# Three rotary operations from VectorE to GpSimd in another form, and the last output bank summed as two halves

## Chip, cores and metric

One core of a Trainium2 chip runs the whole layer. The metric is the device time of one execution in microseconds (us). Five engines work side by side, each with its own queue, which it takes in order: TensorE (PE, its weight loads PEld), VectorE (DVE), ScalarE (ACT), GpSimd (POOL) and SyncE (SP), which issues most of the loads and stores. TensorE writes its results into PSUM, which is used here as eight banks of 128 x 512 floats.

## What is computed

One decoder layer on 256 tokens of width 1024. All of it is float32.

```python
xn = rms_norm(h, norm_mix_g)
proj = jnp.einsum('bsd,de->bse', xn, w_in)
qa, ka, va, c_q, c_kv, k_rope = jnp.split(proj, cuts, axis=-1)
...   # head group A: dilated window attention on rms-normed qa, ka; va
...   # head group B: queries and keys from the latents c_q, c_kv, plus the shared k_rope;
qb = jnp.concatenate([qb[..., :64], apply_rope(qb[..., 64:], positions)], axis=-1)
kb = jnp.concatenate([kb[..., :64], apply_rope(kb[..., 64:], positions)], axis=-1)
...
h = h + jnp.einsum('bse,ed->bsd', mixed, w_o)
hn = rms_norm(h, norm_ffn_g)
hid = jnp.square(jax.nn.relu(jnp.einsum('bsd,df->bsf', hn, w_ff1)))
h = h + jnp.einsum('bsf,fd->bsd', hid, w_ff2)
```

`apply_rope` needs the cosine and the sine of position times frequency, 256 x 16 angles each.

## The kernel before

The 256 tokens are two tiles of 128 rows (`NT = 2`, index t). Every product is made of three: activations and weights are split into a high part (`his`, `hi`) and a low remainder (`los`, `lo`), and high x high, low x high and high x low are summed in one PSUM bank. Weights come from HBM in chunks (tile `raw`, three buffers), are cut into pieces of up to 1024 columns, and each piece is split by a ScalarE cast (L254) and a VectorE subtraction (L255) into one of five `his` and one of five `los` buffers. A load waits until VectorE has subtracted the last piece of the chunk that held the buffer.

PSUM is shared out as three pools: `acc` (4 banks), `mm` (2) and `sc` (2). The projections sum in `acc` (some in `sc`), transposes go through `mm`, attention scores through `sc`.

TensorE's work up to the feed-forward part is kept in the order of a table written by hand, of which this is the stretch that matters:

```python
c1*5 A1 r0 c1*3 l*2 L0 l*3 x0 l*2 L1 l x1 g*2 y0 x2 g*2 y1 g L2 x3
```

`c1` is a step of the second half of the c_q projection, `l` a step of the c_kv projection, `g` of the va projection (each step six matmuls). `A1` (`stack_heads(1)`) transposes the normed keys of head group A through the two `mm` banks (L163), casts their high part (ACT, L517) and subtracts it for the low part (DVE, L518, four instructions; the first and the third read one bank, the second and the fourth the other). `L0` and `L1` transpose the c_q latent through the same two banks, and split it (ACT L286, DVE L287). `x0`, `x1` are score products with their softmax (DVE L546 and L552, ACT L549), `y0` transposes the first unit's probabilities, so it waits for L552.

`r0` is `rotary_tables`: it reduces the angles by multiples of two pi, folds them into the range where a polynomial holds, and evaluates it, nearly all on GpSimd, on tiles of 128 x 32 (`ang`, `arg`) and 128 x 64 (`sq`, `trig`). GpSimd is kept in program order. Three of the folds, an absolute value (L421), a minimum (L424) and a maximum (L426), stand on VectorE. GpSimd goes on from the tables to the norms of the latents and the rotation of the shared key (`kr`), and then to the factors `s_k`, whose input VectorE makes.

VectorE's and ScalarE's order is set by the framework's scheduler, from its own estimate of times; the kernel gives none. A VectorE instruction that waits for GpSimd holds up all that stands behind it in VectorE's queue.

The feed-forward part goes over 8 blocks of 512 hidden columns: `ff1(n)`, then `ff2(n-1)`, which adds to four banks `f_ps[t][b]` (two of `sc`, two of `mm`; t the rows, b the column half of the output). The last block, `ff2_last(7)`, finishes one bank after the other: twelve matmuls of 512 columns, then VectorE multiplies the bank by the norm's factor and adds the residual (L813), then SP stores it (L814). The last bank, t = b = 1, is added and stored in two halves of 256 columns, after all twelve matmuls.

Of the kernel before, what the change touches and what calls it, by code (L numbers as in the profile page):

```python
# [20 lines left out]
ALU = mybir.AluOpType  # L21
AX = mybir.AxisListType

P = 128
S = 256
NT = S // P
# [11 lines left out]
NFB = DFF // FB  # L38
# [139 lines left out]
def tile_layer(ctx, tc, x, xt, cols_in, rows_in, w_all, out):  # L178
    nc = tc.nc
    V, A, G, T = nc.vector, nc.scalar, InOrder(tc, nc.gpsimd), Products(tc)  # L180
# [14 lines left out]
    acc = ctx.enter_context(tc.tile_pool(name="acc", bufs=4, space=bass.MemoryType.PSUM))  # L195
# [3 lines left out]
    def bank(pool=mm):  # L199
        return pool.tile([P, 512], F32, name=pool.name)  # L200
# [4 lines left out]
    def tiny(n, name, bufs=1):  # L205
        return small.tile([P, n], F32, name=name, bufs=bufs)
# [8 lines left out]
    first = const.tile([P, NFRONT + S], F32, name="first")  # L215
# [4 lines left out]
    xs = [keep.tile([P, DM], F32, name=f"x{t}") for t in range(NT)]  # L220
# [26 lines left out]
    def split_next():  # L247
        i = queue["split"]
        c, r, a, n = PIECES[i]
        while queue["load"] <= c:  # L250
            list(load_next())
        raw = queue["raw"][c][:, r:r + a, :]
        hi, lo = (p.tile([P, PIECE], F32R, name=p.name)[:, :a * n].rearrange("p (a n) -> p a n", a=a) for p in (his, los))
        pinned(A.copy(out=hi, in_=raw))  # L254
        pinned(V.tensor_tensor(out=lo, in0=raw, in1=hi.bitcast(F32), op=ALU.subtract))  # L255
        queue["parts"][i] = hi, lo
        queue["split"] += 1

    def weights(name):

        i = queue["at"]
        assert CHUNKS[PIECES[i][0]][0] == name, (PIECES[i], name)
        if queue["split"] == i:
            split_next()
        queue["at"] += 1
        return queue["parts"].pop(i)
# [41 lines left out]
    def three(outs, act, w, k, j, first, last, cs=slice(None)):  # L308

        hi, lo = act[:2]  # L310
        whi, wlo = (z[:, j, cs] for z in w)
        for i, (a, z) in enumerate(((hi, whi), (lo, whi), (hi, wlo))):
            for t in range(NT):
                T.matmul(out=outs[t][:, :whi.shape[1]], lhsT=a[:, k, t * P:(t + 1) * P], rhs=z, start=first and i == 0, stop=last and i == 2)

    def project_steps(name, act, k0, n, done, pool=acc):


        ps = [bank(pool) for _ in range(NT)]
        j = 0  # L320
        while j < n:
            w = weights(name)
            for i in range(w[0].shape[1]):
                three(ps, act, w, k0 + j, i, j == 0, j == n - 1)
                j += 1
                if j == n:
                    done(ps)
                yield
# [62 lines left out]
    def rotary_tables():  # L391
        ang = [const.tile([P, NT, HR], F32, name=f"ang{i}") for i in range(4)]
        pos = const.tile([P, NT], F32, name="pos")
        V.tensor_copy(out=pos, in_=first[:, F_POS:F_POS + NT].bitcast(I32))
        a0, kh, kl, r = ang
        full = [P, NT, HR]
        inv = first[:, F_INV:F_INV + HR]
        G.tensor_tensor(out=a0, in0=pos.unsqueeze(2).broadcast_to(full), in1=inv.unsqueeze(1).broadcast_to(full), op=ALU.mult)

        def two_step(out, in0, scalar, in1, op0, op1):  # L400
            tmp = tiny(NT * ROPE, "rot2", bufs=2)[:, :math.prod(in0.shape[1:])]
            tmp = tmp.rearrange("p (t f) -> p t f", t=NT) if len(in0.shape) == 3 else tmp
            G.tensor_scalar(out=tmp, in0=in0, scalar1=scalar, scalar2=None, op0=op0)
            G.tensor_tensor(out=out, in0=tmp, in1=in1, op=op1)

        def turns(out, in_, period):
            G.tensor_scalar(out=out, in0=in_, scalar1=1.0 / period, scalar2=MAGIC, op0=ALU.mult, op1=ALU.add)
            G.tensor_scalar(out=out, in0=out, scalar1=MAGIC, scalar2=None, op0=ALU.subtract)

        def less(out, in_, k, part):  # L410
            two_step(out=out, in0=k, scalar=-part, in1=in_, op0=ALU.mult, op1=ALU.add)

        turns(kh, a0, 2 * math.pi * 4096)
        for part in TWO_PI_HI[:3]:
            less(a0, a0, kh, part)
        less(r, a0, kh, TWO_PI_HI[3])
        turns(kl, r, 2 * math.pi)
        for k, part in ((kl, TWO_PI[0]), (kh, TWO_PI_HI[3]), (kl, TWO_PI[1]), (kh, TWO_PI_HI[4]), (kl, TWO_PI[2]), (kh, TWO_PI_HI[5])):
            less(a0, a0, k, part)
        arg = const.tile([P, NT, 2, HR], F32, name="arg")  # L420
        V.scalar_tensor_tensor(out=r, in0=a0, scalar=-1.0, in1=a0, op0=ALU.mult, op1=ALU.max)  # L421
        G.tensor_scalar(out=arg[:, :, 0, :], in0=r, scalar1=-1.0, scalar2=math.pi / 2, op0=ALU.mult, op1=ALU.add)
        G.tensor_scalar(out=r, in0=a0, scalar1=-1.0, scalar2=math.pi, op0=ALU.mult, op1=ALU.add)
        V.tensor_tensor(out=a0, in0=a0, in1=r, op=ALU.min)  # L424
        G.tensor_scalar(out=r, in0=a0, scalar1=-1.0, scalar2=-math.pi, op0=ALU.mult, op1=ALU.add)
        V.tensor_tensor(out=arg[:, :, 1, :], in0=a0, in1=r, op=ALU.max)  # L426
        af = arg.rearrange("p t c f -> p (t c f)")
        sq = const.tile([P, NT * ROPE], F32, name="sq")
        trig = const.tile([P, NT, 2, HR], F32, name="trig")
        tf = trig.rearrange("p t c f -> p (t c f)")  # L430
        G.tensor_tensor(out=sq, in0=af, in1=af, op=ALU.mult)
        G.tensor_scalar(out=tf, in0=sq, scalar1=SIN[6], scalar2=None, op0=ALU.mult)
        for c in SIN[5:0:-1]:
            two_step(out=tf, in0=tf, scalar=c, in1=sq, op0=ALU.add, op1=ALU.mult)
        two_step(out=tf, in0=tf, scalar=1.0, in1=af, op0=ALU.add, op1=ALU.mult)
        for i in range(2):
            tab_c = const.tile([P, NT, ROPE], F32, name=f"tabc{i}")
            tab_s = const.tile([P, NT, ROPE], F32, name=f"tabs{i}")
            g1, g2 = (cols[:, C_ROPE + i * ROPE + z * HR:C_ROPE + i * ROPE + (z + 1) * HR].unsqueeze(1).broadcast_to(full) for z in range(2))
            cos, sin = trig[:, :, 0, :], trig[:, :, 1, :]  # L440
            G.tensor_tensor(out=tab_c[:, :, 0:HR], in0=cos, in1=g1, op=ALU.mult)
            G.tensor_tensor(out=tab_c[:, :, HR:], in0=cos, in1=g2, op=ALU.mult)
            two_step(out=tab_s[:, :, 0:HR], in0=sin, scalar=-1.0, in1=g2, op0=ALU.mult, op1=ALU.mult)
            G.tensor_tensor(out=tab_s[:, :, HR:], in0=sin, in1=g1, op=ALU.mult)
            tabs.append((tab_c, tab_s))
# [273 lines left out]
    for b in range(2):  # L719
# [3 lines left out]
    single = {  # L723
        "A": stack_heads,
        "r": lambda i: rotary_tables(),
        "b": lambda i: spread_bias(),
        "x": begin_a,
# [23 lines left out]
    f_ps, hid = [], {}  # L751
# [40 lines left out]
    def ff2(n):  # L792
        if n == 0:
            f_ps.extend([bank(pool) for _ in range(2)] for pool in (sc, mm))
        for kk in range(4):
            w = weights("ff2")
            for b in range(2):
                three([f_ps[t][b] for t in range(NT)], hid[n], w, kk, 0, n + kk == 0, False, slice(b * 512, (b + 1) * 512))

    def ff2_last(n):  # L800

        ws = [weights("ff2") for _ in range(4)]
        hi, lo = hid[n]
        for b in range(2):
            for t in range(NT):
                ts, cs = slice(t * P, (t + 1) * P), slice(b * 512, (b + 1) * 512)
                for kk, (whi, wlo) in enumerate(ws):
                    for i, (a, w) in enumerate(((hi, whi), (hi, wlo), (lo, whi))):
                        T.matmul(out=f_ps[t][b], lhsT=a[:, kk, ts], rhs=w[:, 0, cs], start=False, stop=kk == 3 and i == 2)
                cut = 256 if b == t == 1 else 512  # L810
                for c0 in range(0, 512, cut):
                    o = xs[t][:, b * 512 + c0:b * 512 + c0 + cut]
                    V.scalar_tensor_tensor(out=o, in0=f_ps[t][b][:, c0:c0 + cut], scalar=r2[:, t:t + 1], in1=o, op0=ALU.mult, op1=ALU.add)  # L813
                    nc.sync.dma_start(out=out[ts, b * 512 + c0:b * 512 + c0 + cut], in_=o)  # L814

    ssh = tiny(NT, "ssh")
    for n in range(NFB):
        ff1(n)
        if n == 1:
# [4 lines left out]
            r2 = tiny(NT, "r2")  # L824
            rsqrt(r2, ssh, NT)
            G.tensor_tensor(out=r2, in0=r2, in1=r2, op=ALU.mult)
        if n:
            ff2(n - 1)
    ff2_last(NFB - 1)


# [44 lines left out]
```

## Time and profile before

| | |
|---|---|
| time, median of 3 runs (lowest to highest) | 320.17 us (319.86 to 320.26) |
| the profiled execution, and its span in the trace | 320.45 us, 318.6 us |
| TensorE busy | 311.2 us (98%) |
| VectorE busy | 215.7 us (68%) |
| ScalarE busy | 177.9 us (56%) |
| GpSimd busy | 57.8 us (18%) |
| mean DMA rate over the span | 179 GB/s |
| mean granted TensorE clock | 0.994 of full speed |

The span runs from the first to the last instruction in the trace; the execution's time has 1.85 us around it. "Busy" of TensorE includes ends that are modelled, since matmuls overlap: two matmuls of 512 columns start 0.23 us apart and each is drawn 0.39 us long. The granted clock is the share of 2.4 GHz that TensorE was given; 0.50 is its lower level, 1.2 GHz.

### The profile page before, as it was taken

The page shows a single profiled execution, that of the slowest core. Times are in us where ns is not written, and L with a number is a line of the kernel's source. Part 1 is how long each engine was busy: PE and PEld are TensorE (multiplying, and loading weights), DVE is VectorE, ACT ScalarE, POOL GpSimd, SP SyncE. Part 2 cuts the span into 40 slices and gives each one's busy share as a digit, 9 for nine tenths or more (in the row PEclk, how much of TensorE's full clock was granted, in tenths as well). Part 3 has the DMA queues.
Part 4 walks back from the last instruction along what each step waited for, and adds up shares of the span by engine and source line. Part 5 has one row for each costly group of instructions (what it writes and reads, how often), then busy time and mean ns, then how long its engine had stood idle before and what let it go on. Part 6 is the DMA issues. An engine that isn't in the chain of part 4 may idle for free.

```text
span 318.6 us, 4545 instructions
## 1 busy us (share of the span) xinstructions
PE 311.2 (98%) x1646; PEld 266.8 (84%) x1646; DVE 215.7 (68%) x387; ACT 177.9 (56%) x317; POOL 57.8 (18%) x118
## 2 busy tenths in 40 slices
PE   8999997999999999999999999999999999999995
PEld 7887997888988887888888888888888888888883
DVE  3859949987797995637995574774754845846722
ACT  4876657858786774419574454443643643545400
POOL 4045877770372200001000000000000000000000
PEclk9999997999999999999999999999999999999999
DMA  7996992434462561305568565646556465553002
GB/s 225 398 385 192 320 291 77 148 86 145 164 220 67 192 205 66 134 0 189 209 242 286 151 219 174 237 146 217 180 151 244 145 233 168 185 195 132 0 35 99
DMA packets 12326, 56.95 MB, mean 179 GB/s; under 512 B 1384, under 2 KB 3440, under 8 KB 7696
## 3 DMA queue, kind: packets, MB, share of 16 engines
q1 hardware_dynamic: 10560, 54.94, 50.6%
q10 hardware_dynamic: 1744, 1.73, 1.8%
q8 instruction: 13, 0.21, 0.3%
q14 instruction: 9, 0.07, 0.1%
HBM read 55.07 MB, written 1.06 MB: 176 GB/s over the span
## 4 chain that ended last, share of the span: by engine, by line
PE 83%; DVE 5%; POOL 5%; ACT 3%; issue 2%; DVEq 0%; ACTq 0%
PE acc L160 45%; PE sc L160 19%; PE mm L160 15%; PE mm L163 4%; DVE los L255 2%; POOL s_a L174 2%; POOL ang L174 2%; ACT his L254 2%; POOL rot L174 1%; ACT sqs L376 1%; DVE big L518 1%; DVE s_a L472 0%; DVE two L287 0%; DVE half L785 0%; ACT two L286 0%
## 5 line engine op out<-in xcount | busy, mean ns | idle before, releaser
L255 DVE TENSOR_TENSOR los<-raw,his 128x1024 fp32r<-128x1024 f32 (+3 forms) x106 | 121.1, 1150 | 64.5 <-ACT his L254 64.4
L254 ACT CAST his<-raw 128x1024 fp32r<-128x1024 f32 (+3 forms) x106 | 104.2, 991 | 86.7 <-PE acc L160 46.1
L160 PE MATMUL acc<-his,two 128*128 128x512 f32 (+2 forms) x288 | 74.4, 381 | 0.0
L160 PE MATMUL acc<-two,his 128*128 128x512 f32 x240 | 63.1, 393 | 0.2 <-DVE half L785 0.2
L160 PEld LDWEIGHTS acc<-his,two 128*128 128x128 f32 x288 | 52.0, 195 | 6.7 <-issue 0.8
L160 PE MATMUL mm<-his,big 128*128 128x512 f32 x128 | 49.1, 390 | 0.0
L160 PE MATMUL sc<-his,big 128*128 128x512 f32 x128 | 49.0, 389 | 0.0
L160 PEld LDWEIGHTS acc<-two,his 128*128 128x128 f32 x240 | 42.6, 188 | 7.6 <-DVE half L785 0.4
L160 PE MATMUL acc<-los,two 128*128 128x512 f32 (+2 forms) x144 | 41.4, 369 | 0.0
L160 PEld LDWEIGHTS acc<-two,los 128*128 128x128 f32 x240 | 34.5, 190 | 3.4
L160 PE MATMUL acc<-two,los 128*128 128x256 f32 x240 | 35.8, 282 | 0.0
L160 PEld LDWEIGHTS acc<-los,two 128*128 128x128 f32 x144 | 27.0, 193 | 3.7
L160 PEld LDWEIGHTS mm<-his,big 128*128 128x128 f32 x128 | 24.0, 188 | 4.8
L160 PEld LDWEIGHTS sc<-his,big 128*128 128x128 f32 x128 | 24.1, 188 | 4.8
L160 PE MATMUL sc<-los,big 128*128 128x512 f32 x64 | 24.9, 389 | 0.0
L160 PE MATMUL mm<-los,big 128*128 128x512 f32 x64 | 24.9, 389 | 0.0
L549 ACT ACTIVATE half<-half,mx 128x128 f32<-128x128 f32 (+1 forms) x32 | 14.2, 449 | 2.3 <-DVE mx L546 2.3
L784 ACT COPY half<-acc 128x256 f32<-128x256 f32 x30 | 9.8, 374 | 7.8 <-PE acc L160 7.8
L160 PEld LDWEIGHTS mm<-los,big 128*128 128x128 f32 x64 | 12.0, 188 | 2.5
L160 PEld LDWEIGHTS sc<-los,big 128*128 128x128 f32 x64 | 12.0, 188 | 2.5
L788 ACT CAST big<-half 128x512 fp32r<-128x512 f32 x16 | 10.0, 625 | 4.1 <-DVE half L786 4.1
L785 DVE TENSOR_TENSOR half<-acc,half 128x256 f32<-128x256 f32 x30 | 11.4, 418 | 1.3 <-ACT half L784 1.3
(143 smaller groups left out, 317.2 us busy)
## 6 DMA issues: line engine op xcount, KB each, us to landing
raw<-in_weights_dram SPq DMA_DIRECT2D x36, 1024.0 KB, 4.8
raw<-in_weights_dram SPq DMA_DIRECT2D x13, 512.0 KB, 5.6
raw<-in_weights_dram SPq DMA_DIRECT2D x6, 768.0 KB, 4.5
raw<-in_weights_dram SPq DMA_DIRECT2D x2, 576.0 KB, 7.6
x<-in_x_dram SPq DMA_DIRECT2D x2, 512.0 KB, 8.7
big<-vec_d ACTq DMA_DIRECT2D x1, 1024.0 KB, 11.9
big<-in_xt_dram SPq DMA_DIRECT2D x3, 256.0 KB, 7.2
raw<-in_weights_dram SPq DMA_DIRECT2D x2, 384.0 KB, 3.0
```

The lines of the kernel that those rows point to most:

```text
L160: return self._issue(self.tc.nc.tensor.matmul(**kw))
L163: return self._issue(self.tc.nc.tensor.transpose(**kw))
L174: return lambda *a, **kw: self.tc.keep_in_program_order(op(*a, **kw))
L254: pinned(A.copy(out=hi, in_=raw))
L255: pinned(V.tensor_tensor(out=lo, in0=raw, in1=hi.bitcast(F32), op=ALU.subtract))
L376: return A.activation(out=junk[:, :src.shape[1]], in_=src, func=AF.Square, accum_out=dst)
L518: V.tensor_tensor(out=k_st[other, :, i, ts], in0=t3[rs], in1=k_st[rs, :, i, ts].bitcast(F32), op=ALU.subtract)
L549: A.activation(out=sb[:, i, :], in_=sb[:, i, :], func=AF.Exp, scale=-1.0, bias=mx[:, i:i + 1], accum_out=mx[:, 4 + i:5 + i])
L784: A.copy(out=zs, in_=ps[2 * b + i][:, S:])
L785: V.tensor_tensor(out=zs, in0=ps[2 * b + i][:, 0:S], in1=zs, op=ALU.add)
L788: A.copy(out=ht[:, sl, :], in_=s3)
```

## The change

The diff has two parts, and one line in a helper that lets a sum end for some rows alone.

In `rotary_tables` the three VectorE instructions go. The absolute value is made on GpSimd as 2 max(a, 0) - a (two instructions), the minimum of a and r as a - max(a - r, 0) (three), the maximum of a and r as a + max(r - a, 0) (three). So VectorE has three instructions less and GpSimd eight more, all of 128 x 32.

In the last block, the bank `f_ps[1][1]` is closed one block earlier (`last = (1,)` at n = 6): VectorE adds it to the residual at the start of `ff2_last`, and the last block's part of these outputs is summed afresh in two `acc` banks, 256 columns in each, one after the other. Each half is added and stored when its own twelve matmuls are done.

```diff
-                T.matmul(..., start=first and i == 0, stop=last and i == 2)
+                T.matmul(..., start=first and i == 0, stop=(t in last if isinstance(last, tuple) else last) and i == 2)
...
-        V.scalar_tensor_tensor(out=r, in0=a0, scalar=-1.0, in1=a0, op0=ALU.mult, op1=ALU.max)
+        G.tensor_scalar(out=kh, in0=a0, scalar1=0.0, scalar2=2.0, op0=ALU.max, op1=ALU.mult)
+        G.tensor_tensor(out=r, in0=kh, in1=a0, op=ALU.subtract)
         G.tensor_scalar(out=arg[:, :, 0, :], in0=r, scalar1=-1.0, scalar2=math.pi / 2, op0=ALU.mult, op1=ALU.add)
         G.tensor_scalar(out=r, in0=a0, scalar1=-1.0, scalar2=math.pi, op0=ALU.mult, op1=ALU.add)
-        V.tensor_tensor(out=a0, in0=a0, in1=r, op=ALU.min)
+        G.tensor_tensor(out=r, in0=a0, in1=r, op=ALU.subtract)
+        G.tensor_scalar(out=r, in0=r, scalar1=0.0, scalar2=None, op0=ALU.max)
+        G.tensor_tensor(out=a0, in0=a0, in1=r, op=ALU.subtract)
         G.tensor_scalar(out=r, in0=a0, scalar1=-1.0, scalar2=-math.pi, op0=ALU.mult, op1=ALU.add)
-        V.tensor_tensor(out=arg[:, :, 1, :], in0=a0, in1=r, op=ALU.max)
+        G.tensor_tensor(out=r, in0=r, in1=a0, op=ALU.subtract)
+        G.tensor_scalar(out=r, in0=r, scalar1=0.0, scalar2=None, op0=ALU.max)
+        G.tensor_tensor(out=arg[:, :, 1, :], in0=a0, in1=r, op=ALU.add)
...
-                three([f_ps[t][b] for t in range(NT)], hid[n], w, kk, 0, n + kk == 0, False, ...)
+                last = (1,) if b == 1 and n == NFB - 2 and kk == 3 else False
+                three([f_ps[t][b] for t in range(NT)], hid[n], w, kk, 0, n + kk == 0, last, ...)
...
+        add(f_ps[1][1], 1, 512, 512)
+        for t, c0, w in ((0, 0, 512), (1, 0, 512), (0, 512, 512), (1, 512, 256), (1, 768, 256)):
+            ts, cs = slice(t * P, (t + 1) * P), slice(c0, c0 + w)
+            ps = f_ps[t][c0 // 512] if w == 512 else bank(acc)[:, :w]
+            for kk, (whi, wlo) in enumerate(ws):
+                for i, (a, z) in enumerate(((hi, whi), (hi, wlo), (lo, whi))):
+                    T.matmul(out=ps, lhsT=a[:, kk, ts], rhs=z[:, 0, cs], start=w < 512 and kk == i == 0, stop=kk == 3 and i == 2)
+            nc.sync.dma_start(out=out[ts, cs], in_=add(ps, t, c0, w))
```

In the built programs the lines behind the new ones have moved by seven (L518 is L525, L598 is L605). VectorE's queue around the rotary operations, as a difference of the two programs (`big<-mm,big` are the four low parts of the keys, `los` the splits of c_kv weights):

```order
 L255 TENSOR_TENSOR los<-raw,his 128x576 x3
-L421 SCALAR_TENSOR_TENSOR ang_565<-ang_562 128x32
-L424 TENSOR_TENSOR ang_562<-ang_562,ang_565 128x32
-L518 TENSOR_TENSOR big<-mm,big 64x4x128
-L426 TENSOR_TENSOR arg<-ang_562,ang_565 128x2x16
-L518 TENSOR_TENSOR big<-mm,big 64x4x128
+L525 TENSOR_TENSOR big<-mm,big 64x4x128 x2
 L255 TENSOR_TENSOR los<-raw,his 128x576
-L518 TENSOR_TENSOR big<-mm,big 64x4x128 x2
-L598 COPY nats<-acc 128x384 x2
+L525 TENSOR_TENSOR big<-mm,big 64x4x128 x2
+L605 COPY nats<-acc 128x384 x2
```

Nothing between the third split and the four low parts of the keys is left on VectorE; the rest of this stretch keeps its order. GpSimd's queue at the same place:

```order
 L174 TENSOR_TENSOR ang_562<-rot_600,ang_562 128x32
+L174 TENSOR_SCALAR ang_563<-ang_562 128x32
+L174 TENSOR_TENSOR ang_565<-ang_563,ang_562 128x32
 L174 TENSOR_SCALAR arg<-ang_565 128x2x16
-L174 TENSOR_SCALAR ang_565<-ang_562 128x32 x2
+L174 TENSOR_SCALAR ang_565<-ang_562 128x32
+L174 TENSOR_TENSOR ang_565<-ang_562,ang_565 128x32
+L174 TENSOR_SCALAR ang_565<-ang_565 128x32
+L174 TENSOR_TENSOR ang_562<-ang_562,ang_565 128x32
+L174 TENSOR_SCALAR ang_565<-ang_562 128x32
```

Two of the five new instructions of this piece make the absolute value, three the minimum; three more follow for the maximum, and the polynomial (`sq`, `trig`) stands behind them as before. VectorE's last instructions, with the residual `x` of the rows t = 0 (x_112) and t = 1 (x_113):

```order
 L255 TENSOR_TENSOR los<-raw,his 128x1024 x2
-L813 SCALAR_TENSOR_TENSOR x_112<-sc,r_1882,x_112 128x512
-L813 SCALAR_TENSOR_TENSOR x_113<-mm,r_1882,x_113 128x512
-L813 SCALAR_TENSOR_TENSOR x_112<-sc,r_1882,x_112 128x512
-L813 SCALAR_TENSOR_TENSOR x_113<-mm,r_1882,x_113 128x256 x2
-L872 UNCONDITIONAL_BRANCH
+L813 SCALAR_TENSOR_TENSOR x_113<-mm,r_1887,x_113 128x512
+L813 SCALAR_TENSOR_TENSOR x_112<-sc,r_1887,x_112 128x512
+L813 SCALAR_TENSOR_TENSOR x_113<-mm,r_1887,x_113 128x512
+L813 SCALAR_TENSOR_TENSOR x_112<-sc,r_1887,x_112 128x512
+L813 SCALAR_TENSOR_TENSOR x_113<-acc,r_1887,x_113 128x256 x2
```

One addition of 512 columns is new, ahead of the others; the last two read two `acc` banks instead of one `mm` bank. On TensorE the last twelve matmuls of 512 columns become 24 of 256; all its work ahead of them stands in the same order in both programs.

## Rows read from the trace of the kernel before

**Rows 1.** Waits of TensorE from 64 to 315 us: total us, times, longest
```profile
PE mm L163 <- DVE half L552: 0.5, 1, 0.5
PE acc L160 <- DVE half L785: 0.2, 1, 0.2
```

**Rows 2.** TensorE in order of time, 51 to 64 us: start, us, instruction [idle before]
```profile
51.15 1.27 PE L163 MATMUL mm<-ident,nats 128*128 128x128 f32 x6 [1.78 <-DVE big L518]
...
55.94 1.00 PE L160 MATMUL sc<-big,two 128*128 128x128 f32 x8
...
57.63 0.69 PE L160 MATMUL acc<-his,two 128*128 128x288 f32 x4
...
58.42 0.82 PE L163 MATMUL mm<-ident,nats 128*128 128x128 f32 x6
59.00 0.78 PE L160 MATMUL acc<-his,two 128*128 128x288 f32 x4
...
63.80 0.82 PE L163 MATMUL mm<-ident,half 128*128 128x128 f32 x4 [0.53 <-DVE half L552]
```

**Rows 3.** VectorE in order of time, the same columns, 46 to 64 us
```profile
46.81 0.19 DVE L421 SCALAR_TENSOR_TENSOR ang<-ang 128x32 f32<-128x32 f32 x1 [2.92 <-POOL ang L174]
47.65 0.19 DVE L424 TENSOR_TENSOR ang<-ang,ang 128x32 f32<-128x32 f32 x1 [0.64 <-POOL ang L174]
47.87 0.69 DVE L518 TENSOR_TENSOR big<-mm,big 64x512 fp32r<-64x512 f32 x1
...
63.38 0.87 DVE L552 TENSOR_SCALAR half<-half,mx 128x128 f32<-128x128 f32 x4
```

**Rows 4.** ScalarE in order of time, the casts ahead of the first two L518
```profile
44.25 1.06 ACT L517 CAST big<-mm 64x512 fp32r<-64x512 f32 x2 [1.15 <-PE mm L163]
```

**Rows 5.** Stretches: length, busy us of PE PEld DVE ACT POOL, PEclk, DMA share, GB/s
```profile
47.87:63.38 15.51, 13.62 (x84) 12.39 (x82) 14.98 (x36) 12.19 (x32) 12.06 (x28) 0.89 0.35 115
...
52.10:55.00 2.90, 2.90 (x14) 2.90 (x13) 2.87 (x4) 2.67 (x7) 2.65 (x4) 0.50 0.28 113
...
64.00:65.00 1.00, 1.00 (x9) 0.88 (x9) 0.71 (x5) 1.00 (x5) 0.51 (x3) 1.00 0.85 78
```

**Rows 6.** GpSimd in order of time, 46 to 82 us
```profile
46.52 0.25 POOL L174 TENSOR_TENSOR ang<-rot,ang 128x32 f32<-128x32 f32 x1
...
48.86 0.29 POOL L174 TENSOR_TENSOR sq<-arg 128x64 f32<-128x64 f32 x1 [0.72 <-DVE arg L426]
...
52.74 1.42 POOL L174 TENSOR_SCALAR rot<-trig 128x64 f32<-128x64 f32 x1
...
58.15 0.47 POOL L174 TENSOR_TENSOR tabc<-trig,cols 128x32 f32<-128x32 f32 x2
...
71.35 0.37 POOL L174 TENSOR_SCALAR kr<-kr,by_kr 128x32 f32<-128x32 f32 x1
81.89 0.28 POOL L174 TENSOR_SCALAR s_k<-s_k,add_k 128x4 f32<-128x4 f32 x1 [10.17 <-DVE s_k L472]
```

**Rows 7.** VectorE's weight splits, two stretches: ns min/median/max, first and last start
```profile
L255 DVE TENSOR_TENSOR los<-raw,his x5: 1214/1226/1227, 52.7 to 62.2; 128x1024 fp32r<-128x1024 f32 x5
...
L255 DVE TENSOR_TENSOR los<-raw,his x54: 1214/1226/1227, 159.5 to 299.2; 128x1024 fp32r<-128x1024 f32 x54
```

**Rows 8.** TensorE and VectorE in order of time, feed-forward part and end
```profile
176.00 1.12 PE L160 MATMUL acc<-two,los 128*128 128x256 f32 x8
176.95 2.00 PE L160 MATMUL acc<-two,his 128*128 128x512 f32 x8
...
308.15 0.75 DVE L813 SCALAR_TENSOR_TENSOR x<-sc,r,x 128x512 f32<-128x512 f32 x1 [4.97 <-PE sc L160]
...
311.95 0.39 PE L160 MATMUL mm<-his,big 128*128 128x512 f32 x1
...
314.44 0.39 PE L160 MATMUL mm<-his,big 128*128 128x512 f32 x1
...
314.87 0.88 DVE L813 SCALAR_TENSOR_TENSOR x<-mm,r,x 128x256 f32<-128x256 f32 x2 [1.97 <-PE mm L160]
```

More of the change, by code (lines that the diff above doesn't have):

```diff
@@ L313, in three @@
             for t in range(NT):
-                T.matmul(out=outs[t][:, :whi.shape[1]], lhsT=a[:, k, t * P:(t + 1) * P], rhs=z, start=first and i == 0, stop=last and i == 2)
+                T.matmul(out=outs[t][:, :whi.shape[1]], lhsT=a[:, k, t * P:(t + 1) * P], rhs=z, start=first and i == 0, stop=(t in last if isinstance(last, tuple) else last) and i == 2)
     def project_steps(name, act, k0, n, done, pool=acc):
@@ L797, in ff2, with add @@
             for b in range(2):
-                three([f_ps[t][b] for t in range(NT)], hid[n], w, kk, 0, n + kk == 0, False, slice(b * 512, (b + 1) * 512))
+                last = (1,) if b == 1 and n == NFB - 2 and kk == 3 else False
+                three([f_ps[t][b] for t in range(NT)], hid[n], w, kk, 0, n + kk == 0, last, slice(b * 512, (b + 1) * 512))
     def ff2_last(n):
+        def add(ps, t, c0, w):
+            o = xs[t][:, c0:c0 + w]
+            V.scalar_tensor_tensor(out=o, in0=ps, scalar=r2[:, t:t + 1], in1=o, op0=ALU.mult, op1=ALU.add)
+            return o
         ws = [weights("ff2") for _ in range(4)]
         hi, lo = hid[n]
[L804 to L814, printed above, removed]
+        add(f_ps[1][1], 1, 512, 512)
[6 more added lines that the diff above has]
+            nc.sync.dma_start(out=out[ts, cs], in_=add(ps, t, c0, w))
     ssh = tiny(NT, "ssh")
```

## The prediction

> **What bounds the kernel now.** TensorE is busy for 98% of the span, so first I looked for where it is not: the list of its waits. From 64 us on there is next to nothing, 0.5 us for L552 and 0.2 us for L785 [rows 1], the first of which is the wait at 63.80 itself. So after 64 us the time is TensorE's own work in a fixed order, and whatever makes TensorE reach that point earlier makes the end earlier by as much, as long as the engines that feed it come earlier too. The other large wait lies before it: 1.78 us ahead of the transposes at 51.15, released by L518 [rows 2].
>
> Next I read VectorE's queue backwards from that L518. VectorE stands idle for 2.92 us, from 43.89 to 46.81, until GpSimd has an angle ready for L421, again for 0.64 us ahead of L424, and only then comes the first L518 at 47.87 [rows 3]. The low parts of the keys have nothing to do with the angles; they stand behind them in one queue. Their own inputs were there long before: ScalarE's first two casts took 44.25 to 45.31 [rows 4].
>
> Third, the granted clock. Behind that stall TensorE runs at 0.50, its lower level of 1.2 GHz, for 52.10 to 55.00 at least [rows 5]. From the start of the transposes at 51.15 to the start of the scores at 55.94 it needs 4.79 us [rows 2]; that is six transposes and three c_kv steps. At full clock six transposes take 0.58 (58.42 to 59.00) and a step 0.79 (57.63 to 58.42) [rows 2], together 0.58 + 3 x 0.79 = 2.95. So the low clock costs 1.84 us more, and stall and clock together 1.78 + 1.84 = 3.62 us.
>
> Fourth, what is late next. Between the first L518 at 47.87 and L552 at 63.38, VectorE is busy for 14.98 of 15.51 us [rows 3, 5]. So in this stretch VectorE, not TensorE, sets when the first probabilities are ready, and TensorE already waits 0.53 us for them at 63.80 [rows 2]. The gain is therefore the smaller of two: what TensorE saves before 63.80, and what VectorE saves before 63.38.
>
> **The rotary part, on VectorE.** Removed ahead of L552: idle 2.92 + 0.64 and three instructions, two of 0.19 by their rows and a third of the same shape and, by choice, the same length [rows 3], together 4.13 us. What comes back: VectorE is through at 43.89 and the first cast ends about half way through the pair, 44.25 + 0.53, call it 44.85 [rows 4], so it still idles some 0.97. That leaves 3.16. The second L518 then wants the second cast, done at 45.31; the first L518, 0.69 long [rows 3], covers that. Some of the 0.53 us that VectorE is idle between 47.87 and 63.38 [rows 5] may go as well, so VectorE saves 3.16 to 3.69; new short waits for ScalarE could take 0.3 off the lower end. I take 3.3, near the lower end, since the casts and the scores that feed VectorE here come from engines that are now no further ahead than before. L552 then starts at 63.38 - 3.3 = 60.1 and the transposes behind it at 63.80 - 3.3 = 60.5.
>
> On TensorE the stall goes entirely: the third and fourth L518, for which the two banks wait, come some 3 us earlier, the stall is 1.78. Without it I count on no drop of the clock there. TensorE would then reach the transposes of the probabilities 3.62 us earlier, 0.32 more than VectorE, and wait 0.53 + 0.32 = 0.85 us in place of 0.53. If VectorE were not the limit, TensorE could gain at most 3.62 + 0.53 = 4.15. So this part is worth 3.3 us, between 2.9 and 4.15.
>
> **The rotary part, on GpSimd.** Eight instructions of 128 x 32 more. One takes 0.25 us (46.52) where VectorE is idle, and the longest of this helper here 1.42 us (52.74) [rows 6]; I take 0.35 from start to start, nearer the first since they are of its shape. The three waits for VectorE go. Now the stretch from 46.77 to the polynomial at 48.86 takes 2.09; with eleven instructions it takes 11 x 0.35 = 3.85, so all behind it is 1.8 us later. What covers this: GpSimd finishes the shared key at 71.35 + 0.37 and is then idle for 10.17 us until VectorE delivers for `s_k` [rows 6]. VectorE will deliver 3.3 us earlier, so 6.9 us of cover are left, and 1.8 costs nothing. Without that cover each of these microseconds would be one of the end.
>
> VectorE now has work beside GpSimd where it was idle. Its weight splits take 1214 to 1227 ns in 52.7 to 62.2, where GpSimd is busy for most of the time, and the same 1214 to 1227 ns from 159.5 us on, where GpSimd has nothing to do [rows 5, 7]; so I charge VectorE nothing. The Trainium skill speaks against that ("SBUF — State Buffer", Who interferes with whom): of a VectorE instruction with two SBUF inputs and a GpSimd instruction that reads SBUF, the one that comes second is held until the first is done. In the trace the GpSimd half agrees (0.25 against 1.42 us), the VectorE half is not to be seen in these splits. By the rows the term is 0; by the rule it is the third rival's price.
>
> **The tail.** The twelve matmuls of 512 columns start at 311.95 to 314.44, one per 0.226 us, and end at 314.44 + 0.39 = 314.83 [rows 8]. 24 of 256 columns with a weight load each: in the feed-forward part eight of that shape take 0.95 us (176.00 to 176.95), 0.119 each [rows 8], so the last one starts at 311.95 + 23 x 0.119 = 314.69 and ends some 0.29 later, 314.98. Before, two additions of together 0.88 follow, from 314.87 to 315.75 [rows 8]; now one of about half that, from 315.02 to 315.5. Gain 0.25 us; the last store is of the same size in both. Bounds: 0.4 if the halves were streamed at exactly half of 0.226, a loss of 2.3 if a matmul took 0.226 whatever its columns (24 x 0.226 - 12 x 0.226 - 0.44). The row of the same shape is the nearest by far, so 0.25. The new early addition, 0.75 long, falls into VectorE's 4.97 us of idling ahead of 308.15 [rows 8]; the closing of that bank a block earlier moves nothing on TensorE.
>
> **Sum.** 3.3 + 0.25 = 3.55. The profiled execution of 320.45 us would take 316.9; the median of 320.17 lies 0.28 under it, so 316.6 us. Own range 315.6 (4.15 + 0.4) to 317.3 (2.9, nothing at the tail).
>
> **The rivals.**
>
> *The clock falls all the same.* TensorE still idles, about 0.85 us, ahead of the probabilities' transposes. After 1.78 us of idling it was at 0.50, after 0.53 us it stayed at 1.00 (64 to 65 us) [rows 2, 5]. Nothing here shows what 0.85 does; it is nearer to the harmless one. Price as before 1.84: 318.4.
>
> *VectorE is held by GpSimd.* From 44.9 to 60 VectorE issues some seven weight splits beside GpSimd. If each waited for one GpSimd instruction of 0.29 [rows 6], VectorE and with it the gain would lose 2.0: 318.6. Against it stand the equal lengths of [rows 7] and the mere 0.53 us of idling [rows 5]. The section of the Trainium skill named above is what speaks for it.
>
> *GpSimd becomes the bound, and the kernel slower.* From 46.77 to 58.15 GpSimd now has 17 instructions in 11.4 us; it will have 25, beside a busier VectorE. The end comes later than before by 0.2% (0.64 us) once this stretch is 6.9 + 3.55 + 0.64 = 11.1 us longer, 22.5 us, or 0.90 us per instruction. The polynomial's fourteen now take 9.29 us (48.86 to 58.15), 0.66 each [rows 6]; at that rate all 25 take 16.5, 5.1 more, still under the cover. At 1.2 us each, half way between the point and the longest seen with its gap, it would be 18.6 longer and the time 316.6 + 18.6 - 6.9 = 328.3.
>
> *The wait stays where it is.* Some other input of the L518 or of the transposes is late as well, a cast or a bank. The casts' row [rows 4] and the one wait released by L518 speak against it. Only the tail's gain is left: 319.9.
>
> **How the numbers follow.** Forecast 0.77, clock 0.10, port 0.05, wait stays 0.05, GpSimd slower 0.03. The range goes from the forecast's low end to the third rival's price, 315.6 to 318.6: nearly all of the forecast and the first two rivals, 0.85 or so. What a measurement of this kernel can tell from no change is about 0.2%, 0.64 us. Faster by more: 0.77 + 0.10 + 0.05 = 0.92; within: 0.05; slower by more: 0.03.
>
> **What would show it.** Right, if TensorE's list of waits has lost the one for L518, the clock stays at full speed from 47 to 60 us, the first low part of the keys starts near 44.9 and L552 near 60.1, and TensorE waits under 1.2 us ahead of the probabilities. GpSimd's polynomial should start between 50.5 and 52 and its wait for `s_k` shrink to some 5 us without VectorE waiting for GpSimd longer than now. At the end one addition of 256 columns follows the last matmul, whose fellows start 0.12 us apart. Wrong, if the splits beside GpSimd take longer than 1.23 us or VectorE shows new idling between 45 and 60; if the clock drops behind the remaining wait; or if a wait after 64 us appears on TensorE that gives the gain back.

## The result, and the profile after

The kernel with the change takes **316.08 us** (median of four runs, 315.90 to 316.33). The kernel before takes 320.03 in the runs beside it (319.86 to 320.26). The ratio is 0.9877, with a 95% interval of 0.9859 to 0.9894: faster by 3.95 us, between 3.4 and 4.5. Forecast were 316.6 us and a gain of 3.55.

| | before | after |
|---|---|---|
| profiled execution, us | 320.45 | 316.21 |
| its span, us | 318.6 | 314.4 |
| TensorE busy, us (matmuls) | 311.2 (1646) | 308.9 (1658) |
| VectorE busy, us | 215.7 | 216.1 |
| GpSimd busy, us (instructions) | 57.8 (118) | 62.7 (126) |

The engines did not get less to do. What went is idling, and a stretch at low clock. The granted TensorE clock after, in 40 slices of the span:

```profile
PEclk9999999999999999999999999999999999999999
```

The seventh slice of the clock was a 7 before; now all are full. All of TensorE's waits in the changed kernel (total us, times, longest):

```profile
PE sc L160 <- DVE touch L212: 1.2, 1, 1.2
PE mm L163 <- DVE half L559: 0.8, 1, 0.8
PE acc L160 <- DVE half L792: 0.2, 1, 0.2
```

The wait of 1.78 for the low parts of the keys (L518, now L525) is no longer in the list, and the one for the probabilities (L552, now L559) grew from 0.53 [rows 1, 2] to 0.8. VectorE after, in order of time (start, us, instruction, idle before):

```profile
44.35 1.28 DVE L525 TENSOR_TENSOR big<-mm,big 64x512 fp32r<-64x512 f32 x2 [0.97 <-ACT big L524]
...
48.87 2.41 DVE L255 TENSOR_TENSOR los<-raw,his 128x1024 fp32r<-128x1024 f32 x2
...
59.42 0.93 DVE L559 TENSOR_SCALAR half<-half,mx 128x128 f32<-128x128 f32 x4
```

The idle time ahead of the first low part is 0.97 us, released by ScalarE's cast, where it was 2.92 and 0.64 released by GpSimd [rows 3]. TensorE after, in the same columns:

```profile
5.46 1.57 PE L160 MATMUL acc<-his,two 128*128 128x512 f32 x4
...
7.32 1.07 PE L160 MATMUL acc<-his,two 128*128 128x512 f32 x4
...
48.44 0.43 PE L160 MATMUL acc<-los,two 128*128 128x288 f32 x2
48.71 0.82 PE L163 MATMUL mm<-ident,nats 128*128 128x128 f32 x6
49.28 0.78 PE L160 MATMUL acc<-his,two 128*128 128x288 f32 x4
...
51.74 1.00 PE L160 MATMUL sc<-big,two 128*128 128x128 f32 x8
...
54.22 0.81 PE L163 MATMUL mm<-ident,nats 128*128 128x128 f32 x6
54.80 0.78 PE L160 MATMUL acc<-his,two 128*128 128x288 f32 x4
...
59.84 0.89 PE L163 MATMUL mm<-ident,half 128*128 128x128 f32 x4 [0.81 <-DVE half L559]
```

The transposes at 48.71 no longer wait. Six of them and the three steps behind take 51.74 - 48.71 = 3.03 us, against 4.79 before [rows 2]; the prediction had worked out 2.95 for full clock.

**Where the 4.24 us between the two profiled executions arise.** Not all of them belong to the change. This is TensorE before, in the first 8 us, where the two programs are alike:

```profile
5.46 2.05 PE L160 MATMUL acc<-his,two 128*128 128x512 f32 x4
...
7.82 1.08 PE L160 MATMUL acc<-his,two 128*128 128x512 f32 x4
```

The same group of four starts at 7.32 after and at 7.82 before, 0.50 apart; two more traces of the kernel before (below) have it at 7.58 and 7.05. That varies from one execution to the next. The offset stays as it is until the rotary part: VectorE's instruction ahead of the low parts ends at 43.38 after, at 43.89 before. So 0.51 is taken off every start below.

| place | before | after | earlier by | without the 0.51 |
|---|---|---|---|---|
| first low part of the keys | 47.87 | 44.35 | 3.52 | 3.01 |
| scores, TensorE | 55.94 | 51.74 | 4.20 | 3.69 |
| probabilities, VectorE | 63.38 | 59.42 | 3.96 | 3.45 |
| their transposes, TensorE | 63.80 | 59.84 | 3.96 | 3.45 |
| first matmul of the last bank | 311.95 | 308.06 | 3.89 | 3.38 |
| end of the last addition | 315.75 | 311.61 | 4.14 | 3.63 |

The gain of the rotary part is complete at 59.84 and then stands still for 250 us; the tail adds the rest. Of TensorE's 3.69 at the scores, 0.24 are lost again in its longer wait for VectorE: VectorE's 3.45 is the smaller, and it is what stays.

The tail after, matmuls and additions of the last bank and of its halves:

```profile
300.18 0.75 DVE L813 SCALAR_TENSOR_TENSOR x<-mm,r,x 128x512 f32<-128x512 f32 x1 [0.89 <-PE mm L160]
...
308.06 0.28 PE L160 MATMUL acc<-his,big 128*128 128x256 f32 x1
309.69 0.48 DVE L813 SCALAR_TENSOR_TENSOR x<-acc,r,x 128x256 f32<-128x256 f32 x1 [0.68 <-PE acc L160]
310.81 0.28 PE L160 MATMUL acc<-his,big 128*128 128x256 f32 x1
311.13 0.48 DVE L813 SCALAR_TENSOR_TENSOR x<-acc,r,x 128x256 f32<-128x256 f32 x1 [0.95 <-PE acc L160]
```

Twenty-four matmuls start from 308.06 to 310.81, (310.81 - 308.06) / 23 = 0.120 us apart; in [rows 8] it was 0.119 for that shape. From the first of them to the end of the last addition it is 311.61 - 308.06 = 3.55 us, against 315.75 - 311.95 = 3.80: 0.25, the forecast figure. The new early addition, of all blocks but the last (300.18, 0.75 long), stands eight microseconds ahead of that, where VectorE has time.

### The profile page after: what moved, and what is told of

It is laid out like the page before. It is cut to its first block, busy times and chain, and to the rows that moved or that the text cites. A ratio compares the mean times of both kernels' runs of the same rounds, so it can differ in the third digit from the quotient of the medians.

```text
span 314.4 us, 4576 instructions
## 1 busy us (share of the span) xinstructions
PE 308.9 (98%) x1658; PEld 265.8 (85%) x1658; DVE 216.1 (69%) x385; ACT 177.9 (57%) x317; POOL 62.7 (20%) x126
## 3 DMA queue, kind: packets, MB, share of 16 engines
q1 hardware_dynamic: 10560, 54.94, 50.5%
## 4 chain that ended last, share of the span: by engine, by line
PE 90%; DVE 5%; ACT 3%; issue 1%; DVEq 0%; ACTq 0%
PE acc L160 49%; PE sc L160 22%; PE mm L160 14%; PE mm L163 4%; DVE los L255 2%; ACT his L254 2%; ACT sqs L376 1%; ACT two L286 1%; DVE big L525 1%; DVE half L553 0%; DVE two L287 0%; DVE half L792 0%; DVE nats L615 0%; DVE half L793 0%; DVE nats L605 0%
## 5 line engine op out<-in xcount | busy, mean ns | idle before, releaser
L160 PE MATMUL acc<-his,two 128*128 128x512 f32 (+2 forms) x288 | 72.8, 374 | 0.0
L160 PEld LDWEIGHTS acc<-his,two 128*128 128x128 f32 x288 | 50.7, 190 | 6.6 <-issue 0.8
L160 PE MATMUL mm<-his,big 128*128 128x512 f32 x120 | 46.5, 390 | 0.0
L160 PEld LDWEIGHTS acc<-los,two 128*128 128x128 f32 x144 | 26.3, 188 | 3.6
L160 PEld LDWEIGHTS mm<-his,big 128*128 128x128 f32 x120 | 22.6, 188 | 4.5
L160 PE MATMUL mm<-los,big 128*128 128x512 f32 x60 | 23.3, 389 | 0.0
L160 PEld LDWEIGHTS mm<-los,big 128*128 128x128 f32 x60 | 11.3, 188 | 2.4
L286 ACT ACTIVATE two<-mm,cols 128x256 fp32r<-128x256 f32 x16 | 7.3, 472 | 8.9 <-PE mm L163 8.1
```

What stands on the lines that cost most here:

```text
L160: return self._issue(self.tc.nc.tensor.matmul(**kw))
L286: a = pinned(A.activation(out=hi, in_=src, func=AF.Copy, scale=g))
```

## The experiments

All are compared with the kernel before, run beside them on the same chip. "Low parts" are the four subtractions that L518 issues, "probabilities" the scaling at L552 and the transposes that wait for it.

### Each part alone

The first kernel is the kernel before with the rotary hunk of the diff alone, the second with the hunks of the last bank alone.

> The kernel before with the rotary part of the change alone. Theory (VectorE's queue was blocked behind the angles): nearly the whole gain, 3.3 to 3.7 us, so 316.3 to 316.7 beside a kernel before of 320.0; TensorE's wait for the low parts of the keys gone, clock at full speed from 47 to 60 us. Rival (the tail carries half or more of the gain): 318 or later.

> The kernel before with the halves of the last bank alone. Theory: 0.25 us, so 319.7 to 319.8 beside 320.0, with the stretch from the first matmul of the last bank to the end of the last addition at 3.55 us in place of 3.80; the stall at 51 us and the low clock behind it unchanged. Rival (the tail carries half or more of the gain): 318 or earlier.

The rotary part alone takes 316.29 us, a ratio of 0.9894 (0.9879 to 0.9909), 3.4 us less. The tail alone takes 319.38 against 319.76, a ratio of 0.9988 (0.9979 to 0.9997), 0.38 us less, with an interval from 0.1 to 0.7 that holds the forecast 0.25. Together 3.8 of the 3.95. The tail's own trace has its first matmul at 311.39 and its last addition here:

```profile
311.39 0.28 PE L160 MATMUL acc<-his,big 128*128 128x256 f32 x1
...
314.46 0.48 DVE L807 SCALAR_TENSOR_TENSOR x<-acc,r,x 128x256 f32<-128x256 f32 x1 [0.95 <-PE acc L160]
```

314.94 - 311.39 = 3.55, the same as in the changed kernel.

The tail-only trace also showed something unexpected. Up to the feed-forward part this is the program of before, and the low clock was expected behind its stall. It has the same stall, but not the same clock. TensorE in order of time, and a window (length, busy us of PE PEld DVE ACT POOL, granted clock, DMA share, GB/s):

```profile
50.67 1.02 PE L163 MATMUL mm<-ident,nats 128*128 128x128 f32 x6 [1.77 <-DVE big L519]
...
57.83 0.44 PE L163 MATMUL mm<-ident,nats 128*128 128x128 f32 x2 [0.84 <-DVE two L287]
...
63.26 0.83 PE L163 MATMUL mm<-ident,half 128*128 128x128 f32 x4 [0.96 <-DVE half L553]
...
50.60:53.00 2.40, 2.33 (x18) 2.17 (x19) 2.34 (x4) 1.28 (x4) 2.06 (x5) 1.00 0.62 218
```

Behind 1.77 us of idling the clock is at 1.00, the level of 2.4 GHz, where the profile of before had 0.50, that of 1.2 GHz, behind 1.78 [rows 2, 5]. And TensorE is no earlier for it: from the stalled transposes to the probabilities' it takes 63.26 - 50.67 = 12.59 us, before 63.80 - 51.15 = 12.65. What it does not lose to the clock it waits for VectorE, 0.84 and 0.96 us.

### Was the low clock worth anything?

That puts in doubt the 1.84 us that the prediction charged to the clock. Two more profiled executions of the unchanged kernel before:

> The kernel before once more, for its trace. In the profile that the prediction read, the clock was at 0.50 behind the 1.78 us stall; behind the same stall of the kernel with the tail part alone it stayed at full speed. Theory (VectorE sets when the probabilities' transposes start, so the low clock cost nothing): from the stalled transposes to the probabilities' transposes 12.6 us, whichever clock follows the stall; with full clock TensorE waits some 1.8 us more in between. Rival (the low clock is part of the gain): 12.6 us with the low clock and 10.8 us without.

> The same as the run above, once more, since which clock follows the stall is not in the program: 12.6 us from the stalled transposes to the probabilities' transposes by the theory, 10.8 us by the rival if the clock stays at full speed.

They took 320.27 and 319.59 us. TensorE in the first:

```profile
48.89 0.43 PE L160 MATMUL acc<-los,two 128*128 128x288 f32 x2
51.08 1.02 PE L163 MATMUL mm<-ident,nats 128*128 128x128 f32 x6 [1.76 <-DVE big L518]
51.85 0.77 PE L160 MATMUL acc<-his,two 128*128 128x288 f32 x4
...
54.31 1.00 PE L160 MATMUL sc<-big,two 128*128 128x128 f32 x8
...
56.79 0.60 PE L163 MATMUL mm<-ident,nats 128*128 128x128 f32 x4
58.22 0.44 PE L163 MATMUL mm<-ident,nats 128*128 128x128 f32 x2 [0.83 <-DVE two L287]
58.42 0.78 PE L160 MATMUL acc<-his,two 128*128 128x288 f32 x4
...
63.65 0.83 PE L163 MATMUL mm<-ident,half 128*128 128x128 f32 x4 [0.96 <-DVE half L552]
```

and in the second:

```profile
50.42 1.02 PE L163 MATMUL mm<-ident,nats 128*128 128x128 f32 x6 [1.76 <-DVE big L518]
...
63.00 0.82 PE L163 MATMUL mm<-ident,half 128*128 128x128 f32 x4 [0.98 <-DVE half L552]
```

Both kept full clock behind the same stall, and both need 12.57 and 12.58 us for the stretch. So it is some 12.6 us with the low clock and without it; the theory that VectorE sets the length holds, and the rival of 10.8 us falls. The 0.7 us between the two executions is there at 51.08 against 50.42 already.

The runs without a trace have a mean granted clock each. The trace with the fall has 0.994, those of before without it 0.998. Of the 34 runs of the kernel before that stand beside the seven changed kernels of this section, three are at 0.994 or 0.995; they took 319.69, 320.19 and 320.37 us, the other 31 took 319.43 to 320.36. The mean doesn't say where in a run the clock fell, but the three lie among the others and not 1.84 us above them.

A kernel that fills the stall was to show the same from the other side: before, with fourteen identity transposes that nobody reads ahead of the stalled ones.

```
+        if fill:
+            idle = bank(sc)
+            for i in range(fill):
+                T.transpose(out=idle[:, (i % 4) * P:(i % 4 + 1) * P], in_=ident, identity=ident)
...
-        "L": lambda i: transposed_split(..., *cT[:2]),
+        "L": lambda i: transposed_split(..., *cT[:2], fill=14 if i == 0 else 0),
```

> The kernel before with 14 transposes of the identity, which nothing reads, put on TensorE ahead of the stalled transposes, some 1.5 us of the 1.78 us stall; VectorE keeps its rotary operations and its idle time, but the framework's scheduler takes one weight split out of VectorE's way ahead of L552. Theory (the low clock comes from the idling; and the gain is the smaller of what TensorE and VectorE save): the clock stays at full speed behind the filler, so the scores x0 start near 54.1 in place of 55.9, but the first probabilities come when VectorE has them, 62.2 to 63.4 in place of 63.4, so 318.8 to 320.0. Rival (TensorE's lost time alone counts): 318.2. If the longer wait ahead of the probabilities' transposes lowers the clock in turn: 1.8 us later than either.

It takes 320.81 us, a ratio of 1.0019 (1.0002 to 1.0036): by that nothing is gained. But the median mixes two groups of runs. Six of the ten have a mean granted clock of 0.995 and took 320.8 to 321.3 us; the other four, at 0.998 to 1.000, took 319.3 to 319.7, about 0.3 less than the 319.80 of before. TensorE in the profiled execution, one of the six, and a window:

```profile
50.40 1.01 PE L163 MATMUL mm<-ident,nats 128*128 128x128 f32 x6 [0.23 <-DVE big L522]
...
62.79 0.63 PE L163 MATMUL mm<-ident,half 128*128 128x128 f32 x4 [1.86 <-DVE two L287]
...
64.00:66.00 2.00, 2.00 (x6) 1.54 (x5) 2.00 (x9) 1.11 (x4) 1.70 (x5) 0.50 0.43 127
```

The stall is gone (0.23 left), the clock is full up to 60 us, and TensorE reaches the probabilities only to idle for 1.86 us there. 62.79 - 50.40 = 12.39, nearly the same again. So without the stall, and with the clock full, the runs lie where the theory had them (318.8 to 320.0) and not at the rival's 318.2. Here the clock fell behind that second idling, and at this place, where no later wait hides it, it did cost: the two groups are some 1.6 us apart, the third case of the expectation, which had put it at 1.8. The experiment is not a clean one: with the fill the program's scheduler also puts a weight split behind the scaling of the probabilities. The scaling comes earlier by that, and the wait at 62.79 ends on L287, another instruction of VectorE; so the 0.3 us are not the fill's alone.

### The engine or the place in the queue?

The rotary hunk does two things: it takes three instructions off VectorE, and it lets VectorE go past the wait for GpSimd. To part them, the three instructions stay on VectorE in their old form, and are only issued behind the last low part.

```
-        V.scalar_tensor_tensor(out=r, in0=a0, scalar=-1.0, in1=a0, op0=ALU.mult, op1=ALU.max)
+        with tc.issue_after(low_done[0]):
+            V.scalar_tensor_tensor(out=r, in0=a0, scalar=-1.0, in1=a0, op0=ALU.mult, op1=ALU.max)
...
-                    V.tensor_tensor(out=k_st[other, :, i, ts], ...)
+                    low_done[:] = [V.tensor_tensor(out=k_st[other, :, i, ts], ...).ins]
```

(the other two in the same way)

> The kernel before with the three rotary operations still on VectorE, in their old form, but held in its queue until the fourth low part of the keys (L518) has been issued. Theory (the place in the queue is what cost the time, not the engine): VectorE saves the idle 2.92 and 0.64 less the 0.97 that remains, some 2.6 us, and keeps 0.57 us of the three operations, so 317.2 to 317.5. Rival (what counts is that the folds are on GpSimd, without the hops between the engines): the gain stays under 1 us, 319.0 or later.

317.04 us, a ratio of 0.9911 (0.9897 to 0.9924), 2.85 us less: five sixths of what the rotary hunk brings, and a little more than the 317.2 to 317.5 expected. VectorE in order of time:

```profile
44.49 1.28 DVE L523 TENSOR_TENSOR big<-mm,big 64x512 fp32r<-64x512 f32 x2 [0.97 <-ACT big L522]
...
47.96 0.19 DVE L422 SCALAR_TENSOR_TENSOR ang<-ang 128x32 f32<-128x32 f32 x1
...
50.26 0.19 DVE L426 TENSOR_TENSOR ang<-ang,ang 128x32 f32<-128x32 f32 x1
```

The low parts have the same 0.97 us of idling ahead of them as in the changed kernel, and the three instructions come without a wait, since GpSimd is long done. Their own time, three of 0.19, is about the 0.54 us by which the gain falls short of the rotary hunk's; the two intervals are too wide to show more.

### How far GpSimd's cover reaches

Into the changed kernel, between the last new instruction and the polynomial, go 8 and 24 multiplications by one of 128 x 32, on a tile that nobody reads afterwards:

```
+        for _ in range(8):
+            G.tensor_scalar(out=kl, in0=kl, scalar1=1.0, scalar2=None, op0=ALU.mult)
```

> The changed kernel with eight more GpSimd instructions of 128 x 32 between the folds and the polynomial, whose results nothing reads. They add 2.6 us at 0.33 each to some 4.8 at 0.6 each. Theory (GpSimd's wait for s_k, 3.63 us in the changed kernel, is cover): no change, 316.0 to 316.4. Rival (GpSimd beside VectorE holds VectorE up, or the cover is less than the wait shows): 0.5 us or more later.

> The changed kernel with 24 such instructions, 8 to 14 us. Theory: the cover of 3.63 us is exceeded, VectorE waits for s_k and TensorE for the keys of head group B; later by up to 4 to 10 us, less what slack TensorE has behind s_k, which nothing shows: 317 to 326. Rival (GpSimd cannot become the bound here): 316.1.

With 8 the time is 316.07, no different from the changed kernel. With 24 it is 320.76, 4.7 us later than that, a ratio to before of 1.0028 (1.0017 to 1.0039). GpSimd's wait for `s_k` is 3.63 us in the changed kernel (below) and 1.7 with 8. With 24, where the waits of VectorE, TensorE in order of time and a window read:

```profile
DVE nats L696 <- POOL s_k L174: 5.6, 4, 3.1
...
92.27 1.09 PE L163 MATMUL mm<-ident,nats 128*96 128x128 f32 x4 [2.85 <-ACT pts L576]
...
92.00:94.00 2.00, 1.73 (x7) 1.71 (x8) 2.00 (x6) 1.80 (x4) 1.92 (x2) 0.50 0.20 76
```

VectorE now waits 5.6 us in four waits for GpSimd's `s_k`, where in the kernel before and in the changed one it is 1.6 in two; TensorE stands for 2.85 us ahead of transposes at 92 us, and the clock falls behind that. So the rival "GpSimd becomes the bound" exists, but not with the eight instructions of the change: with instructions of this kind it begins somewhere between sixteen more, those of the change among them, and thirty-two.

### What the remaining wait is worth

The changed kernel still idles for 0.81 us on TensorE ahead of the probabilities. In the table that sets TensorE's order, one step `g` of the c_kv projection is moved ahead of those transposes:

```
-... l x1 g*2 y0 x2 g*2 y1 g L2 ...
+... l x1 g*3 y0 x2 g y1 g L2 ...
```

> The changed kernel with one va projection step (six matmuls, 1.39 us) moved from behind to ahead of the transposes of the first unit's probabilities. Theory (after the change VectorE is what TensorE waits for there, 0.81 us, and nothing after that binds): the wait is filled and the time falls by up to 0.8 us, 315.3 to 315.6 beside 316.1. Rival (the feeders behind that point are as late as VectorE, so the wait moves to the next transposes): no change, 316.0 to 316.2.

314.92 us (314.67 to 315.05), a ratio to before of 0.9848 (0.9834 to 0.9861): 4.85 us less than before and less than the changed kernel by 0.9 (from the ratios) to 1.2 us (from the medians), the best of all here. That is somewhat beyond the 0.8 us expected; with intervals of this width the two can't be told apart. TensorE:

```profile
59.74 0.62 PE L160 MATMUL acc<-los,two 128*128 128x512 f32 x2
60.19 0.60 PE L163 MATMUL mm<-ident,half 128*128 128x128 f32 x4
```

No idle time is left ahead of the transposes. They start no earlier than in the changed kernel, but one step of work stands before them and no longer behind.

## Why the prediction was right, and where it was not

**VectorE's account: right.** Idle time ahead of the first low part: 0.97 forecast, 0.97 measured. Its start, with the profiled execution's 0.51 put back: 44.85 forecast, 44.86 measured. At the probabilities 3.3 was taken, from 3.16 to 3.69; measured 3.45, which is 0.29 more than the plain 3.16. The stretch from the first low part to the probabilities took 15.51 us before [rows 5] and 59.42 - 44.35 = 15.07 after, with VectorE busy for 14.64 of it. So its other idling there went from 0.53 only to 0.43, and 0.10 of the 0.29 come from there; its busy time fell by 14.98 - 14.64 = 0.34, which is 0.15 more than the third instruction's 0.19. The last 0.04 lie ahead of the first low part. TensorE's new wait: 0.85 forecast, 0.81 measured.

**The rule "the smaller of two": right, but one of the two was wrong.** TensorE's side was put at 1.78 + 1.84 = 3.62, stall and low clock, and as that lay so near to VectorE's 3.3, it looked as if both engines gained alike. But the 1.84 did not reach the end. In three of four traces of this stretch (the tail alone changes nothing in it) the clock did not fall, and it took 12.6 us in all four. The step that failed is "the low clock costs 1.84 us more": that is a cost to TensorE's own work, and here VectorE makes TensorE wait for most of that time anyway. It was also too large. From the stalled transposes to the scores it is 54.31 - 51.08 = 3.23 us at full clock in the first of the two further traces, so of the 4.79 with the low clock 1.56 are the clock's; the rest of the 1.84 is a slower start behind the stall, whatever the clock.

What TensorE does lose is to be read from the first of the two further traces, at full clock, from the last step ahead of the stall to the probabilities: 63.65 - 48.89 = 14.76 us, and 59.84 - 48.44 = 11.40 in the changed kernel, 3.36 less. Around the stalled transposes it is 51.85 - 48.89 = 2.96 against 49.28 - 48.44 = 0.84, so 2.12 (the stall of 1.76 and a slower start behind it); around the next transposes, with the wait for L287, 58.42 - 56.79 = 1.63 against 54.80 - 54.22 = 0.58, so 1.05; and the last wait is 0.96 against 0.81. These three make 3.3 of the 3.36, all of them at waits for VectorE. They come to nearly the sum with the clock in it. The forecast held because it took VectorE's 3.3, the smaller, and that did not rest on the clock; that the profile of before caught one of the few executions with the fall, and so gave TensorE a sum of about the right size, was luck. The stall alone, 1.78, would have named TensorE as the smaller side. With the clock out of it, what bounds the stretch is VectorE, from one end to the other.

**The clock behind the remaining wait: the rival did not come.** It stayed at full speed behind 0.81 us in the changed kernel, as in the kernel with the rotary part alone, and behind 1.0 in the one with the three instructions behind the low parts.

**GpSimd's instructions: mis-sized.** Eight more at 0.35 each was the term, eleven in 3.85 us. GpSimd after, in order of time:

```profile
46.01 0.56 POOL L174 TENSOR_TENSOR ang<-rot,ang 128x32 f32<-128x32 f32 x1
...
49.08 1.09 POOL L174 TENSOR_SCALAR ang<-ang 128x32 f32<-128x32 f32 x1
50.26 1.14 POOL L174 TENSOR_TENSOR ang<-ang,ang 128x32 f32<-128x32 f32 x1
51.49 0.28 POOL L174 TENSOR_SCALAR ang<-ang 128x32 f32<-128x32 f32 x1
...
52.19 0.29 POOL L174 TENSOR_TENSOR sq<-arg 128x64 f32<-128x64 f32 x1
...
78.01 0.28 POOL L174 TENSOR_SCALAR s_k<-s_k,add_k 128x4 f32<-128x4 f32 x1 [3.63 <-DVE s_k L479]
```

From 46.57 to the polynomial at 52.19 it is 5.62 us, 0.51 per instruction. Nine take 0.22 to 0.34, near the 0.25 of the row before, and at 0.35 from start to start that part of the estimate holds; two take 1.09 and 1.14, and they end, at 50.17 and 51.40, about when VectorE's two weight splits of 48.87 end (the second at 51.28, the first half of that stretch earlier, near 50.1). The estimate took the price of an instruction from a stretch in which VectorE stood idle, and the change is what ends that idling. So two of the signs failed: with the 0.51 put back the polynomial starts at 52.70, not between 50.5 and 52, and the wait for `s_k` shrank to 3.63, not to "some 5". It cost nothing: VectorE waits for `s_k` 1.6 us in all, before and after, and the cover held, as the kernels with 8 and 24 more show.

**VectorE beside GpSimd: right.** Its splits, in two stretches of the changed kernel (ns min/median/max, first and last start):

```profile
L255 DVE TENSOR_TENSOR los<-raw,his x5: 1217/1225/1227, 48.9 to 58.3; 128x1024 fp32r<-128x1024 f32 x5
...
L255 DVE TENSOR_TENSOR los<-raw,his x55: 1217/1225/1226, 155.6 to 298.1; 128x1024 fp32r<-128x1024 f32 x55
```

With GpSimd at work and without, they take the same. The Trainium skill has whichever comes second held ("SBUF — State Buffer", Who interferes with whom). Its one half fits the two rows of 1.09 and 1.14 above, by when they end (the prediction's pair of 0.25 and 1.42 us was of two shapes, 128x32 and 128x64, and says less); of its other half, VectorE held by GpSimd, these splits show nothing, and VectorE's 0.43 us of idling in the stretch leave no room for the rival's 2.0. That rival, 318.6, the second in the prediction's list though its text calls it the third, did not come.

**The tail: right to the hundredth** in the trace, 3.80 to 3.55. By the runs' times it is 0.38 (0.1 to 0.7) when made alone.

**The sum.** 3.55 forecast; the profiled pair gives 3.63 without the start-up, the medians 3.95 with an interval from 3.4 to 4.5. The difference of 0.4 is inside that interval, and nothing in the traces asks for another cause.

## What to carry to other kernels

An instruction that waits for a slow engine costs a busy engine not its own 0.19 us but all that stands behind it in the queue. Where it stands in the queue is the first thing to change, and which engine runs it the second: here the place alone gave 2.85 of 3.4 us.

Before charging a low clock or a stall to the end, look one wait further: if the engine's next wait is for a neighbour that is busy all the way, the loss is already covered, and removing it moves little: the filled stall brought 0.3 us while the clock stayed up, and where the new wait behind it let the clock fall, that cost 1.6. After a wait is gone, the next one along is worth a look in the order table: one step moved gave about another microsecond.

A price for a small instruction on GpSimd should be taken from rows in which VectorE works beside it, not from rows in which it idles.

## What the runs showed of the hardware

The granted clock does not answer equal idling equally. Behind 1.76 to 1.78 us of idling at the same place of the same program it was at 0.50 in one trace and at 1.00 in three. Behind 1.86 us (the filled stall) and 2.85 us (24 more on GpSimd) it was at 0.50; behind 0.8 to 1.0 us it stayed at 1.00 in every trace here. The mean clocks of the runs say the same: at or under 0.995 in 3 of 34 runs of the kernel before, in six of ten with the filled stall and in seven of ten with 24 more. What decides it stays open.

The first matmuls of the projections take different times from one execution to the next. The same group of four starts at 7.05, 7.32, 7.58 or 7.82 us, while the rows show TensorE busy without a gap from 5.5 on and the granted clock at 1.00; the cause is not shown. That is up to 0.77 us of a measurement that has nothing to do with any change, more than the tail's whole gain. A pair of single executions of this kernel can't tell such a gain, and the median of repeated runs only just (0.1 to 0.7).
